# Matmul operands at one address modulo 512 bytes, a second bank for the first gate pair, and transposed factors in the block products of a hybrid encoder layer

## The chip, the cores and the metric

The kernel runs on one core of a Trainium2 chip. The metric is the device time of one execution in microseconds, the median of several runs. A core has TensorE (matrix products, its weight loads shown apart as PEld), VectorE (DVE), ScalarE (ACT), GpSimd (POOL), SyncE (SP, which here issues most transfers), an SBUF of 128 partitions and a PSUM of eight banks of 128x512 f32.

## The reference

One layer over 512 tokens of width 1024, all in float32. Cut to what matters:

```
h = rms_norm(x, attn_norm_g)
(a_q, a_ckv, a_iq, a_ik, a_iw, s5_u, c_qkv, c_z, c_a, c_b, gates) = split(h @ w_in)
y_a = dsa_attention(a_q, a_ckv, a_iq, a_ik, a_iw, ...) @ w_proj_a   # index scores, top-128 keys, softmax
y_b = s5_branch(s5_u, ...) @ w_proj_b             # complex diagonal scan, gelu, GLU with w_glu
y_c = gdn_branch(c_qkv, c_z, c_a, c_b, ...) @ w_proj_c   # chunked delta rule, chunks of 64
g_a, g_b, g_c = split(sigmoid(gates))
x = x + (g_a * y_a + g_b * y_b + g_c * y_c) @ w_out
x = x + (silu(conv(h2 @ w_up)[gate]) * conv(h2 @ w_up)[val]) @ w_down   # h2 = rms_norm(x)
return rms_norm(x, final_norm_g)
```

In the delta rule each chunk solves (m + I) sol = rhs with a strictly lower triangular m of 64x64.

## The kernel before

**Products in float32r.** Every large product is made of three: an operand is split into a rounded part (h) and a remainder (l), and wh·xh, wh·xl and wl·xh are summed in PSUM. A matmul takes a stationary tile of 128x128 and a moving one of 128x512 (`mm`, L248; `tr`, L251, is a transpose). A weight tile of 128x1024 is loaded by `wload` (L273): SyncE's transfer into a staging buffer w (L280), ScalarE's cast to wh (L256), VectorE's subtraction to wl (L257). w has a ring of two buffers and, in the first half, a third buffer in a pool of its own, w3, which `wload` takes for every third load, by the count `self.wi`.

**PSUM.** `acc` (L238) gives a bank from one of four rings: acc has two banks, sm two, pt three, po one.

**Stages.** First the S5 branch's input u is projected from the scaled x (xh, xl), while the norm is made; then the columns of w_in, one tile of 128 after another, from the normalised hh and hl (8 pieces of 128 rows, so 24 matmuls for a tile), in the order of a table PLAN. `ahead` loads tiles two or three in advance. In between run, interleaved, the S5 scan (`s5_half`, L702 to L719 are its complex arithmetic on VectorE), the index scores and top-k of the attention, the DeltaNet (`gdn_main`) and the projections of the finished branches (`merge`, L1328, which reads a branch from f_h and f_l, made by `fetch`, L1306). The output projection (mh, ml), the FFN (f_hh, f_hl and then ah, al) and the last norm follow. A scheduler that orders the instructions of each engine when the program is built decides the places of the interleaved pieces, and the pools decide the addresses: tiles of a pool lie one behind the other in the order in which they are first asked for, and pools on the left side of SBUF behind those opened before.

**Gates.** `gates` (L1313) projects a tile of gate columns, takes the tanh on ScalarE from PSUM (m_th, L1324) and stores it (gd, L1325). The first two tiles of all are made together by `proj_pair` (L350), matmul by matmul, since both wait for hh and hl to arrive piece by piece.

**Block products of the inverse.** `gdn_main` inverts blocks of 32x32 out of 16x16 ones: fifteen steps (L949, L950) give the inverses X of the diagonal blocks; copies arrange them (X1 and X2, L951 to L954); then T1 = ND[:,1]·X1 and X21 = X2·T1 are made as eight pairs of a multiplication of 128x512 (L958) and a sum over its last axis (L959). L958 reads one factor, and of the first product both, with a stride. Xa and Ya gather the blocks and their transposes (L961 to L968) and go through DRAM (g_xd) to give g_X and g_Y (L980), which TensorE multiplies with g_NT.

Of the kernel before, what the change touches and what calls it, by code (L numbers as in the profile page):

```python
# [10 lines left out]
F32 = mybir.dt.float32  # L11
# [160 lines left out]
NBIG = 5  # L172
PLAN = [27, 28, 29, 30, 31, 21, 22, 32, 33, 34, 35, 36, 37, 38, 39, 40, 41, 42, 43, 44, 8, 9, 10, 11, 4, 5, 6, 7, 12, 13, 14, 15,
# [52 lines left out]
class _K:  # L226
# [46 lines left out]
    def wload(self, src, n=1024, hl=None, extra=False):  # L273
        nc = self.nc
        self.wi += 1
        if self.w3 and self.wi % 3 == 0:
            w = self.w3.tile([128, 1024], F32, tag="w3", name="w", bufs=1)
        else:
            w = self.wp.tile([128, 1024], F32, tag="w", name="w", bufs=2)
# [70 lines left out]
    def proj_pair(self, i):  # L350

        self.ahead(2)
        two, pss = [self.fq.pop(0) for _ in range(2)], [self.acc(), self.acc()]
# [266 lines left out]
    def s5_main(self):  # L620
# [4 lines left out]
        for z in range(2):  # L625
# [3 lines left out]
            self.sri.append(x)  # L629
        self.s5q = []  # L630
# [185 lines left out]
    def gdn_main(self):  # L816
# [119 lines left out]
        X, X2, X1, T1, X21 = w3(0, 256, 16), w3(256, 512, 16), w3(512, 640, 8), w3(640, 768, 8), w3(768, 896, 8)  # L936
# [4 lines left out]
        nc.gpsimd.memset(Ya[up, :, h0_], 0.0)  # L941
# [4 lines left out]
        nc.sync.dma_start(ND[up, 1], nv[:, h0_, h1_])  # L946
        for i in range(1, 16):
# [3 lines left out]
        nc.vector.tensor_copy(X1[lo], X[lo, :, 0:8])  # L951
        nc.scalar.copy(X1[up], X[lo, :, 8:16])
# [3 lines left out]
        for dst, a, b in ((T1, ND[:, 1].rearrange("p j i -> p i j"), X1), (X21, X2, T1)):  # L956
            for c in range(0, 16, 4):
                tt(t4, _bc(a[:, c:c + 4], 2, 8), _bc(b.rearrange("p j k -> p k j"), 1, 4), OP.mult)  # L958
                nc.vector.tensor_reduce(dst[:, c:c + 4], t4, AX.X, OP.add)  # L959
        tr_ = lambda x: x.rearrange("p i k -> p k i")  # L960
        nc.scalar.copy(Xa[lo, :, h0_], X[lo])  # L961
        nc.scalar.copy(Xa[up, :, h1_], X[up])
        nc.scalar.copy(Ya[lo, :, h0_], tr_(X[lo]))
# [342 lines left out]
    def fetch(self, d):  # L1306
        h = self.fp_.tile([128, 4, 512], F32R, tag="fh", name="f_h")
        l = self.fp_.tile([128, 4, 512], F32R, tag="fl", name="f_l")
# [48 lines left out]
    def run(self):  # L1357
# [3 lines left out]
        self.sm = ctx.enter_context(self.pool("sm", bufs=2))  # L1361
        self.dp = ctx.enter_context(self.pool("dp", bufs=1, space=DRAM))
# [13 lines left out]
        with ExitStack() as mix:  # L1376
            wst = mix.enter_context(ExitStack())
            self.wp = wst.enter_context(self.pool("wp", bufs=2))
            mpl = mix.enter_context(self.pool("mix", bufs=1))
# [5 lines left out]
            self.ab = mpl.tile([128, 4, 12], F32, tag="ab", name="ab")  # L1385
# [4 lines left out]
            with ExitStack() as s:  # L1390
# [4 lines left out]
                self.s5e = s.enter_context(self.pool("s5e", bufs=1))  # L1395
                hs = ExitStack()
                hp = hs.enter_context(self.pool("hp", bufs=1))
                sync = nc.sync.dma_start
                ag = hp.tile([128, 8], F32, tag="ag", name="ag")
# [298 lines left out]
```

## Time and profile before

| quantity | value |
| --- | --- |
| median of 3 runs | 937.7 us (935.88 to 937.9) |
| profiled execution | 937.33 us, of it span 935.5 us |
| mean granted TensorE clock | 0.992 |
| TensorE busy | 914.2 us, 98% |
| VectorE busy | 646.1 us, 69% |
| ScalarE busy | 414.4 us, 44% |
| GpSimd busy | 62.7 us, 7% |
| moved by DMA | 114.55 MB |

The span is the time from the first to the last instruction of the profiled execution. In the timeline a row is an instruction with its start, its duration, its engine, line and operation, the tile written and the tiles read, and in brackets the idle time of its engine before it and what ended that. Matmuls overlap, so a row of 0.39 us is not a pace: the pace is the distance between two starts. The chain of waits joins instructions that follow each other without a wait into pieces with a count, so duration by count is a pace as well.

### The profile page before, as it was taken

The page shows a single profiled execution, that of the slowest core. Times are in us where ns is not written, and L with a number is a line of the kernel's source. Part 1 is how long each engine was busy: PE and PEld are TensorE (multiplying, and loading weights), DVE is VectorE, ACT ScalarE, POOL GpSimd, SP SyncE. Part 2 cuts the span into 40 slices and gives each one's busy share as a digit, 9 for nine tenths or more (in the row PEclk, how much of TensorE's full clock was granted, in tenths as well). Part 3 has the DMA queues.
Part 4 walks back from the last instruction along what each step waited for, and adds up shares of the span by engine and source line. Part 5 has one row for each costly group of instructions (what it writes and reads, how often), then busy time and mean ns, then how long its engine had stood idle before and what let it go on. Part 6 is the DMA issues. An engine that isn't in the chain of part 4 may idle for free.

```text
span 935.5 us, 12723 instructions
## 1 busy us (share of the span) xinstructions
PE 914.2 (98%) x4804; PEld 744.2 (80%) x4804; DVE 646.1 (69%) x1136; ACT 414.4 (44%) x753; POOL 62.7 (7%) x103
## 2 busy tenths in 40 slices
PE   8989999999999999899999999999999999999996
PEld 6768877788887778788777889888888888888885
DVE  6988498989999779467768545866666666522423
ACT  7467454244575634258733224534443443321212
POOL 3121001021003200400100000000000000000000
PEclk9999999999999999899999999999999999999999
DMA  9585323342335644631147513423223323232312
GB/s 341 179 208 150 105 95 114 119 147 90 101 103 136 166 119 150 191 124 37 45 135 234 205 46 113 136 90 110 94 90 100 103 90 94 87 113 91 103 55 90
DMA packets 48269, 114.55 MB, mean 122 GB/s; under 512 B 13712, under 2 KB 15120, under 8 KB 48080
## 3 DMA queue, kind: packets, MB, share of 16 engines
q1 hardware_dynamic: 40144, 96.76, 32.0%
q0 software_dynamic: 4032, 9.97, 4.4%
q10 hardware_dynamic: 4032, 7.01, 2.1%
q8 instruction: 38, 0.62, 0.3%
q14 instruction: 23, 0.19, 0.1%
HBM read 94.84 MB, written 14.42 MB: 117 GB/s over the span
## 4 chain that ended last, share of the span: by engine, by line
PE 84%; DVE 9%; issue 3%; DMA 2%; ACT 1%; SPq 1%; POOL 0%; POOLq 0%; DVEq 0%; ACTq 0%
PE ps_acc L248 43%; PE ps_sm L248 22%; PE ps_pt L248 13%; PE ps_po L248 4%; DVE wl L257 1%; PE ps_pt L251 1%; DMA sq<-in_x_dram 1%; PE ps_sm L251 1%; DMA w<-in_w_glu_dram 1%; DVE g_xt L958 1%; DVE g_W L959 1%; DVE a_p L1256 0%; DVE s_rd L710 0%; DVE ht L1491 0%; DVE hl L257 0%
## 5 line engine op out<-in xcount | busy, mean ns | idle before, releaser
L257 DVE TENSOR_TENSOR wl<-w,wh 128x1024 fp32r<-128x1024 f32 (+1 forms) x140 | 168.9, 1207 | 137.7 <-ACT wh L256 137.4
L256 ACT CAST wh<-w 128x1024 fp32r<-128x1024 f32 (+1 forms) x140 | 145.5, 1040 | 231.2 <-PE ps_acc L248 126.5
L248 PE MATMUL ps_acc<-hh,wh 128*128 128x512 f32 x376 | 151.2, 402 | 3.4 <-ACT m_th L1324 2.9
L248 PE MATMUL ps_acc<-hh,wl 128*128 128x512 f32 x376 | 150.4, 400 | 0.0
L248 PE MATMUL ps_acc<-hl,wh 128*128 128x512 f32 x376 | 149.2, 399 | 0.0
L248 PEld LDWEIGHTS ps_acc<-hh,wh 128*128 128x128 f32 x376 | 70.9, 188 | 21.4 <-ACT m_th L1324 3.3
L248 PEld LDWEIGHTS ps_acc<-hh,wl 128*128 128x128 f32 x376 | 71.0, 189 | 17.5 <-issue 1.2
L248 PEld LDWEIGHTS ps_acc<-hl,wh 128*128 128x128 f32 x376 | 70.9, 189 | 16.8 <-issue 1.1
L248 PE MATMUL ps_acc<-f_hh,wh 128*128 128x512 f32 x160 | 62.3, 389 | 0.0
L248 PE MATMUL ps_acc<-f_hl,wh 128*128 128x512 f32 x160 | 62.3, 389 | 0.0
L248 PE MATMUL ps_acc<-f_hh,wl 128*128 128x512 f32 x160 | 62.2, 389 | 0.0
L248 PE MATMUL ps_sm<-f_hh,wh 128*128 128x512 f32 x160 | 62.2, 389 | 0.0
L248 PE MATMUL ps_sm<-f_hl,wh 128*128 128x512 f32 x160 | 62.2, 389 | 0.0
L248 PE MATMUL ps_sm<-f_hh,wl 128*128 128x512 f32 x160 | 62.2, 389 | 0.0
L256 ACT CAST ah<-f_th 128x512 fp32r<-128x512 f32 x22 | 13.6, 620 | 57.6 <-DVE f_th L1629 57.6
L248 PEld LDWEIGHTS ps_sm<-f_hh,wh 128*128 128x128 f32 x160 | 30.1, 188 | 6.3
L248 PEld LDWEIGHTS ps_acc<-f_hl,wh 128*128 128x128 f32 x160 | 30.0, 188 | 6.3
L248 PEld LDWEIGHTS ps_sm<-f_hl,wh 128*128 128x128 f32 x160 | 30.0, 188 | 6.2
L248 PEld LDWEIGHTS ps_acc<-f_hh,wl 128*128 128x128 f32 x160 | 30.1, 188 | 6.2
L248 PEld LDWEIGHTS ps_acc<-f_hh,wh 128*128 128x128 f32 x160 | 30.0, 187 | 6.2
L248 PEld LDWEIGHTS ps_sm<-f_hh,wl 128*128 128x128 f32 x160 | 30.0, 187 | 6.2
L1627 ACT ACTIVATE f_th<-f_a 128x512 f32<-128x512 f32 x22 | 13.9, 632 | 45.2 <-DVE f_a L1624 45.2
(553 smaller groups left out, 1941.6 us busy)
## 6 DMA issues: line engine op xcount, KB each, us to landing
w<-in_w_in_dram SPq DMA_DIRECT2D x50, 512.0 KB, 3.5
w<-in_w_up_dram SPq DMA_DIRECT2D x44, 512.0 KB, 3.3
w<-in_w_down_dram SPq DMA_DIRECT2D x22, 512.0 KB, 3.3
gd<-m_th ACTq DMA_DIRECT2D x24, 256.0 KB, 2.1
m_th<-gd SPq DMA_DIRECT2D x24, 256.0 KB, 3.6
w<-in_w_out_dram SPq DMA_DIRECT2D x8, 512.0 KB, 3.9
sq<-in_x_dram SPq DMA_DIRECT2D x4, 512.0 KB, 9.0
w<-in_w_proj_b_dram SPq DMA_DIRECT2D x4, 512.0 KB, 3.8
```

Of the source, the lines that this page charges most:

```text
L248: return self.nc.tensor.matmul(out, lhsT, rhs, start=start, stop=stop)
L251: return self.nc.tensor.transpose(out, in_, self.ident[base:base + n, base:base + n])
L256: self.lasta = nc.scalar.copy(hi, src)
L257: self.lastv = nc.vector.tensor_sub(lo, src, hi.bitcast(F32))
L958: tt(t4, _bc(a[:, c:c + 4], 2, 8), _bc(b.rearrange("p j k -> p k j"), 1, 4), OP.mult)
L959: nc.vector.tensor_reduce(dst[:, c:c + 4], t4, AX.X, OP.add)
L1627: nc.scalar.activation(th, tl[0], AF.Tanh)
```

## The change

- Pads and another order of the pools and tiles (a pad of 112 columns in s5e, a second of 112 in s5, one of 24 on the right side, `ab` in the pool sm, xh and xl first in hp, f_h and f_l allocated once in a pool opened before gs). With them the stationary and the moving operand of nearly all 512-column float32r products begin at the same byte address modulo 512.
- The second tile of the first gate pair takes a bank of the ring pt instead of acc.
- `wload` takes the third staging buffer at another phase of its count.
- In the block products ND[:,1] is first copied in transposed order (NDt, into Ya's place), and X1 and T1 are kept transposed, so that the multiplications read along unit strides. Ya's zeros are written later.

```diff
+S5PAD = 112
@@ wload
-        if self.w3 and self.wi % 3 == 0:
+        if self.w3 and self.wi % 3 == 2:
@@ proj_pair
-        two, pss = [self.fq.pop(0) for _ in range(2)], [self.acc(), self.acc()]
+        two, pss = [self.fq.pop(0) for _ in range(2)], [self.acc(), self.acc("pt")]
@@ s5
+        self.s5.tile([128, 112], F32, tag="pad2", name="s5_pad2", bufs=1)
@@ gdn_main
-        X, X2, X1, T1, X21 = w3(0, 256, 16), w3(256, 512, 16), w3(512, 640, 8), w3(640, 768, 8), w3(768, 896, 8)
+        X, X2, X21 = w3(0, 256, 16), w3(256, 512, 16), w3(768, 896, 8)
+        X1, T1 = w3(512, 640, 16), w3(640, 768, 16)
...
-        nc.gpsimd.memset(Ya[up, :, h0_], 0.0)
...
+        NDt = Ya.rearrange("p (z a) b -> p z (a b)", z=2)[:, 0].rearrange("p (i j) -> p i j", i=16)
+        nc.scalar.copy(NDt, ND[:, 1].rearrange("p j i -> p i j"))
...
-        nc.vector.tensor_copy(X1[lo], X[lo, :, 0:8])
-        nc.scalar.copy(X1[up], X[lo, :, 8:16])
+        tr_ = lambda x: x.rearrange("p i k -> p k i")
+        nc.vector.tensor_copy(X1[lo], tr_(X[lo, :, 0:8]))
+        nc.scalar.copy(X1[up], tr_(X[lo, :, 8:16]))
...
-        for dst, a, b in ((T1, ND[:, 1].rearrange("p j i -> p i j"), X1), (X21, X2, T1)):
+        for dst, a, b in ((tr_(T1), NDt, X1), (X21, X2, T1)):
             for c in range(0, 16, 4):
-                tt(t4, _bc(a[:, c:c + 4], 2, 8), _bc(b.rearrange("p j k -> p k j"), 1, 4), OP.mult)
+                tt(t4, _bc(a[:, c:c + 4], 2, 8), _bc(b, 1, 4), OP.mult)
...
+        nc.gpsimd.memset(Ya[up, :, h0_], 0.0)
@@ fetch
-        h = self.fp_.tile([128, 4, 512], F32R, tag="fh", name="f_h")
-        l = self.fp_.tile([128, 4, 512], F32R, tag="fl", name="f_l")
+        h, l = self.fh
@@ run
+        self.ab = self.sm.tile([128, 4, 12], F32, tag="ab", name="ab", bufs=1)
+        rpad = ctx.enter_context(self.pool("rpad", bufs=1, side="right"))
+        rpad.tile([128, 24], F32, tag="pad", name="rpad")
...
-            mpl = mix.enter_context(self.pool("mix", bufs=1))
...
-            self.ab = mpl.tile([128, 4, 12], F32, tag="ab", name="ab")
...
+                self.s5e.tile([128, S5PAD], F32, tag="pad", name="s5_pad", bufs=1)
...
+                xh = hp.tile([128, 8, 512], F32R, tag="xh", name="xh")
+                xl = hp.tile([128, 8, 512], F32R, tag="xl", name="xl")
...
-                xh = hp.tile([128, 8, 512], F32R, tag="xh", name="xh")
-                xl = hp.tile([128, 8, 512], F32R, tag="xl", name="xl")
...
+                self.fp_ = s.enter_context(self.pool("fob", bufs=1))
+                self.fh = [self.fp_.tile([128, 4, 512], F32R, tag="f" + z, name="f_" + z) for z in "hl"]
                 self.gs = s.enter_context(self.pool("gs", bufs=1))
-                self.fp_ = s.enter_context(self.pool("fob", bufs=1))
```

Where the tiles lie in the two programs, as the pools place them (bytes modulo 512, moving operand less stationary one):

| moving operand | matmuls with 512 columns | before | after |
| --- | --- | --- | --- |
| hh, hl (input projection) | 1,128 | 224 or 416 | 0 |
| mh, ml (output projection) | 192 | 288 | 0 |
| g_oh, g_ol; a_qh, a_ql (with w) | 96; 96 | 320 | 0 |
| xh, xl (u of the S5 branch) | 99 | 192 or 384 | 0 |
| a_ch, a_cl; a_kd, a_kl | 24; 16 | 96 or 192; 416 | 0 |
| f_h, f_l; f_hh, f_hl; ah, al; iq | 96; 960; 528; 8 | 0 | 0 |
| s_glw; g_rows and w_ik | 48; 29 | unequal | unequal |

The equal ones begin at byte 192 of 512 before (iq's at 480), all at 384 after.

The scheduler puts some pieces in other places. On TensorE, at the end of the first gate pair (ps_acc and ps_pt are banks of the two rings, hh and hl the normalised input, wh and wl a weight tile), before:

```order
L248 MATMUL ps_acc<-hh,wh 128x512
L248 MATMUL ps_acc<-hh,wl 128x512
L248 MATMUL ps_acc<-hh,wh 128x512
L248 MATMUL ps_acc<-hh,wl 128x512
L248 MATMUL ps_acc<-hl,wh 128x512 x2
L248 MATMUL ps_acc<-hh,wh 128x512
L248 MATMUL ps_acc<-hl,wh 128x512
```

and now (here ps_pt is the pair's second tile, ps_acc its first or the third tile):

```order
L249 MATMUL ps_pt<-hh,wl 128x512
L249 MATMUL ps_pt<-hl,wh 128x512
L249 MATMUL ps_acc<-hh,wh 128x512
L249 MATMUL ps_acc<-hh,wl 128x512
L249 MATMUL ps_acc<-hl,wh 128x512
L249 MATMUL ps_pt<-hh,wh 128x512
L249 MATMUL ps_pt<-hh,wl 128x512
L249 MATMUL ps_pt<-hl,wh 128x512
L249 MATMUL ps_acc<-hl,wh 128x512
L249 MATMUL ps_acc<-hh,wl 128x512
L249 MATMUL ps_acc<-hh,wh 128x512
```

Before, the last rows of the pair stand ahead of the first row of the third tile; now most matmuls of the third tile stand between those of the pair.

On TensorE, at the first use of g_X, the inverse (a_ch and a_cl are the attention's latent, f_h and f_l the branch that is being merged), before:

```order
L248 MATMUL ps_acc<-wh,a_ch 128x512
L248 MATMUL ps_acc<-wl,a_ch 128x512
L248 MATMUL ps_acc<-wh,a_cl 128x512
L248 MATMUL ps_sm<-g_X,g_NT 128x64 x8
L248 MATMUL ps_acc<-f_h,wh 128x512
L248 MATMUL ps_acc<-f_l,wh 128x512
L248 MATMUL ps_acc<-f_h,wl 128x512
L248 MATMUL ps_acc<-f_h,wh 128x512
```

and now:

```order
L249 MATMUL ps_acc<-f_h,wl 128x512
L249 MATMUL ps_acc<-f_h,wh 128x512
L249 MATMUL ps_acc<-f_l,wh 128x512
L249 MATMUL ps_acc<-f_h,wl 128x512
L249 MATMUL ps_acc<-f_h,wh 128x512
L249 MATMUL ps_acc<-f_l,wh 128x512
L249 MATMUL ps_acc<-f_h,wl 128x512
L249 MATMUL ps_pt<-a_kd,a_qh 128x128
L249 MATMUL ps_sm<-g_X,g_NT 128x64 x8
L249 MATMUL ps_pt<-a_kd,a_ql 128x128
L249 MATMUL ps_pt<-a_kd,a_qh 128x384
```

The eight products of g_X (16 instructions in the trace) stood ahead of the 12 products of the merge's fourth tile (the rows with f_h and f_l into ps_acc); now they stand behind them and behind one product of the attention.

On VectorE, at the end of the block products (m_th of L1344, now L1349, is the merge's multiplication, which reads a bank that TensorE fills), before:

```order
L959 TENSOR_REDUCE g_W<-g_xt 128x32
L809 SCALAR_TENSOR_TENSOR g_k<-g_k,ps_acc 128x512
L257 TENSOR_TENSOR a_wkl<-w,a_wkh 128x512
L965 COPY g_Xa<-g_W 64x16x8
L966 COPY g_Xa<-g_W 64x16x8
L967 COPY g_Ya<-g_W 64x8x16
L968 COPY g_Ya<-g_W 64x8x16
L1344 SCALAR_TENSOR_TENSOR m_th<-m_th,ps_pt 128x512 x2
L257 TENSOR_TENSOR wl<-w,wh 128x512
L1344 SCALAR_TENSOR_TENSOR m_th<-m_th,ps_pt 128x512
```

and now:

```order
L964 TENSOR_TENSOR g_xt<-g_W 128x512
L258 TENSOR_TENSOR a_wkl<-w,a_wkh 128x512
L1349 SCALAR_TENSOR_TENSOR m_th<-m_th,ps_pt 128x512
L965 TENSOR_REDUCE g_W<-g_xt 128x32
L1349 SCALAR_TENSOR_TENSOR m_th<-m_th,ps_pt 128x512
L971 COPY g_Xa<-g_W 64x16x8
L972 COPY g_Xa<-g_W 64x16x8
L973 COPY g_Ya<-g_W 64x8x16
L974 COPY g_Ya<-g_W 64x8x16
L258 TENSOR_TENSOR wl<-w,wh 128x512
L1349 SCALAR_TENSOR_TENSOR m_th<-m_th,ps_pt 128x512
```

Two of the merge's multiplications stood behind the four copies into g_Xa and g_Ya and now stand ahead of them, as does the subtraction a_wkl, which was ahead already.

On SyncE's queue the transfer of the third tile of w_in now stands ahead of all four loads of x (before, behind three of them), and the two transfers of w_glu stand next to each other. The DeltaNet's small preparations (decay, beta and their logarithms and exponentials) now stand near the S5 branch's first steps, ahead of most of the input projection; before, they stood in its middle.

## Rows read from the trace of the kernel before

**Rows 1.** Page: busy time of each engine, share of the span, instructions.

```profile
PE 914.2 (98%) x4804; PEld 744.2 (80%) x4804; DVE 646.1 (69%) x1136; ACT 414.4 (44%) x753; POOL 62.7 (7%) x103
```

**Rows 2.** Chain of waits: start us, duration us, what, xcount.

```profile
28.23 5.05 PE ps_pt L248 x22
...
269.28 5.60 PE ps_acc L248 x24
...
506.53 2.80 PE ps_acc L248 x12
...
595.95 5.44 PE ps_sm L248 x24
```

**Rows 3.** Timeline of TensorE, f_h and f_l, 370 to 375 us.

```profile
370.02 0.39 PE L248 MATMUL ps_pt<-f_h,wl 128*128 128x512 f32 x1
...
374.79 0.40 PE L248 MATMUL ps_pt<-f_l,wh 128*128 128x512 f32 x1
```

**Rows 4.** Timeline of TensorE at the head and the first gate pair.

```profile
21.48 0.50 PE L248 MATMUL ps_pt<-xh,wl 128*128 128x512 f32 x1 [0.58 <-DVE wl L257]
...
53.37 0.50 PE L248 MATMUL ps_acc<-hh,wh 128*128 128x512 f32 x1 [2.85 <-ACT m_th L1324]
...
54.17 0.63 PE L248 MATMUL ps_acc<-hh,wh 128*128 128x512 f32 x1
...
57.58 0.39 PE L248 MATMUL ps_acc<-hh,wl 128*128 128x512 f32 x1
```

**Rows 5.** Timeline of TensorE and ScalarE at the first use of g_X.

```profile
379.10 0.39 PE L248 MATMUL ps_acc<-wh,a_cl 128*128 128x512 f32 x1
...
381.88 3.65 PE L248 MATMUL ps_sm<-g_X,g_NT 128*128 128x64 f32 x16 [2.39 <-DMA g_X<-g_xd]
...
385.28 0.77 PE L248 MATMUL ps_acc<-f_h,wh 128*128 128x512 f32 x1
...
388.77 0.40 PE L248 MATMUL ps_acc<-f_h,wl 128*128 128x512 f32 x1
...
400.25 2.00 PE L248 MATMUL ps_sm<-g_X,g_NT 128*128 128x64 f32 x16
...
402.06 0.31 PE L248 MATMUL ps_pt<-a_kl,a_ql 128*128 128x128 f32 x1
...
379.52 0.59 ACT L1224 COPY a_V<-ps_acc 128x512 f32<-128x512 f32 x1 [0.74 <-PE ps_acc L248]
```

**Rows 6.** Chain of waits at the S5 scan's end and at g_X.

```profile
134.79 0.35 DVE s_rd L705
...
184.53 0.61 DVE s_si L719
...
379.41 2.33 DMA g_X<-g_xd
```

**Rows 7.** Busy us of each engine by stretch, granted clock, DMA share, GB/s.

```profile
50.00:75.00 25.00, 22.15 (x146) 17.63 (x145) 20.80 (x36) 17.19 (x27) 1.52 (x4) 0.93 0.79 201
...
125.00:150.00 25.00, 25.00 (x199) 18.42 (x199) 25.00 (x50) 11.26 (x17) 0.23 (x2) 1.00 0.28 92
...
200.00:225.00 25.00, 25.00 (x110) 20.16 (x109) 25.00 (x54) 10.08 (x18) 3.04 (x6) 1.00 0.28 99
```

**Rows 8.** Line L958: forms, minimum, median and maximum in ns.

```profile
L958 DVE TENSOR_TENSOR g_xt<-g_ND,g_W x4: 1208/1216/1225, 355.4 to 362.3; 128x512 f32<-128x512 f32 x4
...
L958 DVE TENSOR_TENSOR g_xt<-g_W x4: 1160/1178/1205, 364.3 to 371.6; 128x512 f32<-128x512 f32 x4
```

**Rows 9.** Timeline of VectorE, a multiplication with unit strides.

```profile
48.20 0.68 DVE L580 TENSOR_TENSOR s_tb<-s_fh,cst 128x512 f32<-128x512 f32 x1
```

**Rows 10.** Page: cast and subtraction of weight tiles; their loads.

```profile
L257 DVE TENSOR_TENSOR wl<-w,wh 128x1024 fp32r<-128x1024 f32 (+1 forms) x140 | 168.9, 1207 | 137.7 <-ACT wh L256 137.4
...
L256 ACT CAST wh<-w 128x1024 fp32r<-128x1024 f32 (+1 forms) x140 | 145.5, 1040 | 231.2 <-PE ps_acc L248 126.5
...
w<-in_w_in_dram SPq DMA_DIRECT2D x50, 512.0 KB, 3.5
```

More of the change, by code (lines that the diff above doesn't have):

```diff
@@ L955, in gdn_main @@
         t4 = tmp.rearrange("p (i k j) -> p i k j", i=4, k=8)
-        for dst, a, b in ((T1, ND[:, 1].rearrange("p j i -> p i j"), X1), (X21, X2, T1)):
+        for dst, a, b in ((tr_(T1), NDt, X1), (X21, X2, T1)):
             for c in range(0, 16, 4):
-                tt(t4, _bc(a[:, c:c + 4], 2, 8), _bc(b.rearrange("p j k -> p k j"), 1, 4), OP.mult)
+                tt(t4, _bc(a[:, c:c + 4], 2, 8), _bc(b, 1, 4), OP.mult)
                 nc.vector.tensor_reduce(dst[:, c:c + 4], t4, AX.X, OP.add)
-        tr_ = lambda x: x.rearrange("p i k -> p k i")
         nc.scalar.copy(Xa[lo, :, h0_], X[lo])
         nc.scalar.copy(Xa[up, :, h1_], X[up])
+        nc.gpsimd.memset(Ya[up, :, h0_], 0.0)
         nc.scalar.copy(Ya[lo, :, h0_], tr_(X[lo]))
```

## Prediction

> **What bounds the kernel now.** I read the busy times first: TensorE is busy for 914.2 of 935.5 us and VectorE, the next, for 646.1 [rows 1]. So there are two sources of time only: 21 us in which TensorE stands, and the pace at which it goes. For the pace I took runs of equal 128x512 float32r matmuls out of the chain of waits and divided. In the FFN, 24 take 5.44 us, 226.7 ns each; at the input projection 24 take 5.60 us and at the branch projections 12 take 2.80 us, 233.3 ns each [rows 2]. Same shape, same type, same granted clock, and two paces 6.6 ns apart. The stage isn't the reason: in the middle of the busy DeltaNet stage, products that read f_h and f_l start from 370.02 to 374.79 us 21 intervals apart, 227.1 ns each [rows 3].
>
> What parts the two groups is where the pools put the tiles. Of the 3,320 matmuls with 512 float32r columns, those at 226.7 ns have the moving operand and the stationary one at the same byte address modulo 512 (the FFN, f_h/f_l, ah/al); those at 233.3 ns have them 96 to 224 bytes apart, counted the shorter way round. The products of xh and xl stand between, 22 in 5.05 us, 229.5 ns [rows 2]. In the kernel before 1,592 are equal and 1,728 are not. After the change 3,243 are equal; 77 (w_glu's, rsel's, w_ik's) stay as they were.
>
> Then I looked for TensorE's own waits. Two are large and both also cost clock. At the first pair of gate tiles it stands 2.85 us for the tanh of the first tile, and then 8 matmuls from 54.17 to 57.58 us go at 426 ns, which is the 1.2 GHz level [rows 4]. At the first block products of g_X it stands 2.39 us for a load; the 16 small matmuls then take 3.40 us up to the next start against 1.81 us for the same 16 later, and the 8 intervals behind them 3.49 us [rows 5].
>
> **The change, part by part. Addresses.** 1,552 matmuls move from a 233.3 ns placement to an equal one, 99 (xh, xl) from a 229.5 ns one. 1,552 x 6.6 ns = 10.2 us, 99 x 2.8 ns = 0.3 us: 10.5 us if TensorE alone sets the pace. It does not everywhere. Of the 1,552, 1,128 are the input projection (hh, hl), which lies under 300 us. From 135 to 185.1 us the chain runs mainly through VectorE, and its last link there is s_si, for which TensorE waits [rows 6], and in 125 to 150 and 200 to 225 us VectorE is busy 25.00 of 25 us [rows 7] (225 to 275 us reads the same). About 169 unequal matmuls lie in the first of these stretches: what they gain, 1.1 us, is given back in the wait at 185 us. About 306 lie in 200 to 275 us; TensorE has no wait there now, so VectorE is full but not late, and I take back a third of their 2.0 us, 0.7. That leaves 7.4 - 1.8 = 5.6 us. The other 424 (mh/ml of the output projection, g_oh/g_ol, a_qh/a_ql, a few of the attention's) lie from 375 us on, where VectorE has room: 2.8 us, less 0.2 where they stand before a wait. With xh/xl 8.5 us. The ends: 0 if the pace hangs on something else, 10.5 if all is kept.
>
> The row says that equal and unequal addresses differ by 6.6 ns; that it is the address rather than the tile's place in some other sense is my inference from seven pairs of tiles. The Trainium skill speaks against it: SBUF — State Buffer, section "Who interferes with whom", gives TensorE two independent read ports, one for the moving operand and one for the weight load, and says that "PE and ACT never wait on anyone". By that rule the pads would do nothing; that case is the first rival below.
>
> **First gate pair.** The two tiles of the pair were both in the ring of two banks (tag acc), so the third tile's first matmul waited for the tanh of the first to read its bank. With the second tile in the other ring (tag pt) the third takes the free acc bank, and the order shows it between the pair's own matmuls. TensorE is then never without work: 2.85 us of waiting go, and 8 matmuls go at 2.4 GHz, 3.41 - 8 x 0.233 = 1.55 us [rows 4]. Sum 4.4 us. The tanh is late by nothing new; the next user of the acc ring comes a tile, 5.6 us, later. Ends: 2.85, if another short wait keeps the clock down, and 4.4. If VectorE, which carries the chain up to there, delivers the fourth tile's weights late, part returns; that is in the allowance below.
>
> **Block products.** The 8 multiplies take 1.18 to 1.22 us [rows 8] where a multiply of 128x512 with unit strides took 0.68 us [rows 9]. Unit strides save some 8 x 0.5 = 4 us of VectorE; the extra copy NDt is one ScalarE copy of a size that costs well under 1 us, at a time when ScalarE has gaps. None of that is on TensorE's path as such. What moves the time is the order: the 16 matmuls of g_X now stand behind the 12 of the merge's fourth tile. In the trace g_X's data lands at 379.41 + 2.33 = 381.74 us [rows 6]. TensorE is free at 379.10 + 0.23 = 379.33, waits for the bank that a_V's copy leaves at 380.11 [rows 5], some 0.8 us and 0.1 of slow start, and is through the 12 at 380.2 + 12 x 0.227 = 382.9. That is 1.2 us after the data. The faster products would let the data come earlier, but two of the merge's additions now stand before the Xa/Ya copies and wait for TensorE, so I take 381.7 as it is. So 2.39 us of waiting go, 3.40 - 1.81 = 1.59 us of small matmuls at half clock, and 3.49 - 8 x 0.227 = 1.67 us behind them: 5.65, less 0.9, is 4.8 us. Ends: 1.5 (if the data comes 2 us later than before and half of the clock loss stays) and 5.6.
>
> **Head and staging.** The 0.58 us at 21.48 us is a wait for weights whose transfer stood behind a staging buffer [rows 4]; it now takes the third buffer and is issued before the four loads of x. 0.6 us. The rest of the rotation is shifted by a tile. The DeltaNet's small preparations now run some 200 us earlier, in the stretch where VectorE had 20.80 of 25 us [rows 7]; that, three early activation-table loads and all other reordering I can't cost from rows: -2 to +4 us, taken at 1.0 us lost.
>
> **Sum.** 8.5 + 4.4 + 4.8 + 0.6 - 1.0 = 17.3 us. The profiled run took 937.33 us (span 935.5), 0.4 us under the median 937.7: 937.33 - 17.3 = 920.0 us.
>
> **The rivals.**
> First, *the address is not the cause*: the pace of 233 ns belongs to the projections for another reason, or equality at byte 384, where all operands now lie, is not what equality at 192 was. Then 8.5 us fall out, 937.33 - 9.8 + 1.0 = 928.5 us. Against it speak 233.3 ns for several tiles with different distances and 227.1 for f_h in the same stage [rows 2, 3]. 0.05.
>
> Second, *VectorE becomes the bound of the front part*. It is full where TensorE gets faster [rows 7], and carries the chain up to the first gates and to 185 us. Then everything won before 300 us is given back there: what is left is 250 of the hh/hl matmuls behind 295 us (1.65), the 424 (2.6) and g_X (4.8), 9.0 us: 928.3 us. For it: 25.00 of 25 us busy. Against it: TensorE does not wait from 200 to 275 us. 0.16.
>
> Third, *slower: weights starve*. The rotation of staging buffers is shifted, and the two w_glu loads now stand next to each other on SyncE's queue with the input projection's tiles behind them. A tile that is asked for only when TensorE wants it costs its transfer 3.5, cast 1.04 and subtraction 1.21 us [rows 10], 5.75 us, and some 1.6 us at the lower clock: 7.35 us. It decides from 17.3 / 7.35 = 2.4 tiles; three cost 22.05 us, 942.0 us. In the trace no tile starves so: the waits for weights are 0.58 us and below. 0.04.
>
> Fourth, better than forecast: the waits at 185 us and at the end of the attention shrink as well: 914 or less. 0.03.
>
> **How the numbers follow.** The forecast, with the bounds of its terms 914 to 926 us, has 0.72. The first two rivals lie at 928 to 929, so a range from 913 to 930 leaves out the third, part of the fourth and the tails: it should hold 0.85. About 0.2% is what a measurement of this kernel can tell from no change, 1.9 us. Faster by more: forecast, first, second and fourth, 0.96, less 0.03 for a worse mixture of them: 0.93. Same 0.03, slower 0.04.
>
> **What would show it.** Right: x12 and x24 pieces of the chain at 2.72 and 5.45 us in place of 2.80 and 5.60, at the input, branch and output projections alike; no wait for m_th near 50 us and no 426 ns matmuls behind it; no wait for g_X near 380 us, the 16 small ones in about 1.8 us; granted clock near 1.0 in 50 to 75 and 375 to 400 us; the multiplies at about 0.7 us. Wrong: 233 ns anywhere with equal addresses (first rival); TensorE waits for VectorE between 135 and 300 us that sum to over 4 us (second); waits for wl or wh of over 3 us (third).

## The result and the profile after

The changed kernel takes 923.3 us (median of four runs, 921.6 to 927.3) against 937.1 us of the kernel before: a ratio of 0.986, 95% interval 0.9826 to 0.9893. Measured again beside three experiments it took 922.45 us against 937.65 us, 0.984 (0.9824 to 0.9856). The forecast was 920.0 us, between 913 and 930.

The profiled execution after is the slowest of its four: 927.25 us, span 925.5. The second profile of the same program has a span of 919.4 us, 6.1 us less. The two are runs of one program with one order of instructions. Measured from trace to trace (the start of the last FFN product), the first is 10.1 us ahead of the kernel before and the second 16.2; the sum of the prediction was 17.3.

**Pace.** The chain of waits after (start, duration, what, count), at the input projection and at the branch projections:

```profile
252.22 5.47 PE ps_acc L249 x24
...
497.82 2.72 PE ps_acc L249 x12
```

Where 24 matmuls took 5.60 us and 12 took 2.80 [rows 2], they take 5.47 and 2.72: 227.9 and 226.7 ns each. Over all matmuls of hh and hl the mean distance of two starts (those under 245 ns) fell from 233.1 to 227.9 ns, those of mh and ml from 233.1 to 226.9.

**The block products.** TensorE in the timeline after, where before it waited 2.39 us for g_X [rows 5], and the line of the multiplications (minimum, median, maximum in ns):

```profile
373.56 0.39 PE L249 MATMUL ps_acc<-wh,a_cl 128*128 128x512 f32 x1
374.62 0.50 PE L249 MATMUL ps_acc<-f_h,wh 128*128 128x512 f32 x1 [0.68 <-ACT a_V L1230]
...
377.54 1.95 PE L249 MATMUL ps_sm<-g_X,g_NT 128*128 128x64 f32 x16
379.29 0.31 PE L249 MATMUL ps_pt<-a_kd,a_ql 128*128 128x128 f32 x1
```

```profile
L964 DVE TENSOR_TENSOR g_xt<-g_Ya,g_W x4: 684/692/693, 352.2 to 357.5; 128x512 f32<-128x512 f32 x4
L964 DVE TENSOR_TENSOR g_xt<-g_W x4: 684/688/693, 359.0 to 367.1; 128x512 f32<-128x512 f32 x4
```

The wait for g_X is gone, the new one for a_V's bank is 0.68 us (0.8 was expected), the 16 small products take 1.75 us up to the next start where they took 3.40, and nothing goes at half clock behind them. The multiplications take 0.69 us where they took 1.16 to 1.23 [rows 8].

**New waits.** TensorE's waits after (engine, what it waited to write, for whom, us in all, times, longest):

```profile
PE ps_acc L249 <- DVE sp_l L269: 2.2, 1, 2.2
PE ps_acc L249 <- ACT xh L260: 2.1, 1, 2.1
```

The wait for m_th is gone from the list. In its place stand sp_l (the split of the query projection, which frees a bank; 0.55 us before) and xh at the head (1.15 us before). Both cost more than themselves. The head and the query projection in the timeline after:

```profile
10.22 0.50 PE L249 MATMUL ps_acc<-xh,wh 128*128 128x512 f32 x1 [2.09 <-ACT xh L260]
...
11.81 0.62 PE L249 MATMUL ps_acc<-xl,wh 128*128 128x512 f32 x1
...
15.22 0.41 PE L249 MATMUL ps_acc<-xh,wl 128*128 128x512 f32 x1
```

```profile
290.76 0.47 PE L249 MATMUL ps_acc<-hh,wh 128*128 128x512 f32 x1 [2.19 <-DVE sp_l L269]
...
291.80 0.63 PE L249 MATMUL ps_acc<-hl,wh 128*128 128x512 f32 x1
...
295.17 0.39 PE L249 MATMUL ps_acc<-hh,wh 128*128 128x512 f32 x1
```

Behind each, eight matmuls take 3.4 us, 427 ns each, the 1.2 GHz level: 1.6 us more than at 2.4 GHz. The second profile of the same program has the same places with shorter waits, and no such stretch:

```profile
9.62 0.50 PE L249 MATMUL ps_acc<-xh,wh 128*128 128x512 f32 x1 [1.06 <-ACT xh L260]
...
288.05 0.47 PE L249 MATMUL ps_acc<-hh,wh 128*128 128x512 f32 x1 [1.34 <-DVE sp_l L269]
```

The windows tell the same, first the first profile, then the second (busy us and instructions of PE, PEld, DVE, ACT, POOL; granted clock, DMA share, GB/s):

```profile
0.00:25.00 25.00, 20.81 (x86) 16.96 (x87) 15.49 (x54) 16.76 (x26) 9.19 (x15) 0.93 0.90 338
275.00:300.00 25.00, 22.81 (x104) 18.33 (x103) 21.14 (x51) 12.53 (x26) 7.63 (x14) 0.93 0.53 129
400.00:425.00 25.00, 25.00 (x209) 20.56 (x209) 14.55 (x43) 17.40 (x43) 0.00 (x0) 0.93 0.23 72
```

```profile
0.00:25.00 25.00, 21.41 (x94) 17.05 (x95) 16.08 (x59) 16.98 (x27) 9.22 (x15) 1.00 0.90 337
275.00:300.00 25.00, 23.66 (x115) 19.20 (x114) 23.25 (x52) 13.55 (x25) 10.35 (x18) 1.00 0.64 164
400.00:425.00 25.00, 25.00 (x223) 21.36 (x222) 16.63 (x49) 21.00 (x55) 0.00 (x0) 1.00 0.13 44
```

In the first profile three windows have a clock of 0.93, in the second none. The 6.1 us between them are these: 1.9 at the head (wait and clock together), 2.4 at the query projection, 1.5 around 401 us, where TensorE had no wait but ran small products of 64 and 32 columns, and 0.3 in smaller places.

### The profile page after: what moved, and what is told of

Its sections match the earlier page's. It is cut to its first block, busy times and chain, and to the rows that moved or that the text cites. A ratio compares the mean times of both kernels' runs of the same rounds, so it can differ in the third digit from the quotient of the medians.

```text
span 925.5 us, 12717 instructions
## 1 busy us (share of the span) xinstructions
PE 905.5 (98%) x4804; PEld 744.5 (80%) x4804; DVE 640.5 (69%) x1136; ACT 413.2 (45%) x752; POOL 65.0 (7%) x103
## 4 chain that ended last, share of the span: by engine, by line
PE 86%; DVE 8%; issue 2%; DMA 2%; ACT 1%; POOL 1%; SPq 0%; POOLq 0%; DVEq 0%; ACTq 0%
PE ps_acc L249 44%; PE ps_sm L249 22%; PE ps_pt L249 14%; PE ps_po L249 4%; PE ps_pt L252 1%; DVE wl L258 1%; PE ps_sm L252 1%; DMA w<-in_w_glu_dram 1%; DMA xt<-in_xt_dram 1%; DMA a_ql<-sp_h 1%; DVE a_wk L1141 1%; DVE g_v L798 0%; DVE a_m L1140 0%; DVE s_rb L711 0%; POOL g_orr L371 0%
## 5 line engine op out<-in xcount | busy, mean ns | idle before, releaser
L249 PE MATMUL ps_acc<-hh,wh 128*128 128x512 f32 x368 | 146.0, 397 | 2.2 <-DVE sp_l L269 2.2
L249 PE MATMUL ps_acc<-hl,wh 128*128 128x512 f32 x368 | 145.6, 396 | 0.0
L249 PE MATMUL ps_acc<-hh,wl 128*128 128x512 f32 x368 | 145.4, 395 | 0.0
L1636 ACT ACTIVATE f_th<-f_a 128x512 f32<-128x512 f32 x22 | 13.9, 632 | 45.2 <-DVE f_a L1633 45.2
```

The source lines that it names most:

```text
L249: return self.nc.tensor.matmul(out, lhsT, rhs, start=start, stop=stop)
L1636: nc.scalar.activation(th, tl[0], AF.Tanh)
```

## The experiments

Twelve kernels ran, four at a time on one chip; each ratio is against runs of the kernel before on that chip. The one with matmuls alone ran once and has no ratio. A difference between two kernels of under 2 us lies within the spread of their runs.

### The changed kernel again

> The changed kernel once more, as the yardstick on the chip of the three runs beside it. Expected: 921 to 925 us. Theory A (the profiled run of 927 us was slow because TensorE fell to 1.2 GHz in three stretches, of which only those behind a wait belong to the kernel): the profile shows the waits for xh near 8 to 10 us and for sp_l near 288 us again, with 8 matmuls at 427 ns behind each, but not necessarily the stretch near 401 us, behind which no wait lies. Theory B (all three belong to the program): all three stretches at the same places.

Measured 922.45 us (0.984). The rows are above. Theory A holds, and goes further than it said: the stretches at 1.2 GHz behind the two waits do not belong to the program either. The same program waited 2.19 or 1.34 us for sp_l, 2.09 or 1.06 us for xh, and only the longer ones were followed by half clock.

### hh and hl moved by 128 bytes

```diff
-        rpad.tile([128, 24], F32, tag="pad", name="rpad")
+        rpad.tile([128, 56], F32, tag="pad", name="rpad")
```

> The changed kernel with the right-hand pad 128 bytes wider. The order of the instructions on every engine is the same; only hh, hl and the two tiles beside them move by 128 bytes, so the 1,128 matmuls of hh and hl have their operands 128 bytes apart again. Theory (address decides the pace): those go from about 227.5 to 233 ns, 1,128 x 5.5 to 6.6 ns = 6 to 7.4 us of TensorE, less up to 1.8 us that VectorE hides: 4.5 to 7 us slower than the changed kernel beside it, pieces of 24 in the chain at 5.60 us where they are 5.45. Rival (the pace belongs to the projections' order or stage): the same time as the changed kernel and 227 ns.

Measured 928.82 us (0.9904, 0.9889 to 0.9919), 6.4 us slower than the changed kernel beside it (give or take 2). The order on all five engines is unchanged, so the addresses alone did it. The chain, first of this kernel, then of the changed one at the same tile:

```profile
254.61 5.58 PE ps_acc L249 x24
```

```profile
250.36 5.47 PE ps_acc L249 x24
```

5.58 us is 232.5 ns, 5.47 is 227.9. Over all matmuls of hh and hl the mean rose from 227.9 to 232.6 ns; those of f_h and f_l, which did not move, had 228.3 and now 229.0. The rival of the wrong cause falls. One thing in the expectation is not so: more moved than hh, hl and two tiles. In the changed kernel this pad stays to the end, and mh and ml, which later take the same side of SBUF, lie 128 bytes off as well: their mean rose from 226.8 to 232.7 ns. 1,128 x 4.7 = 5.3 us and 192 x 5.9 = 1.1 us make the 6.4, so no part hidden by VectorE is seen here.

### hh and hl brought to the weights' address in the kernel before

```diff
             right = ExitStack()
+            right.enter_context(self.pool("rpad", bufs=1, side="right")).tile([128, 72], F32, tag="pad", name="rpad")
```

> The kernel before with one pad of 72 columns on the right-hand side and nothing else: the order on all engines is that of before, but for 960 of the 1,128 matmuls of hh and hl both operands now begin at byte 192 of 512; the other 168 stay 192 bytes apart. Theory (address): 960 matmuls at 227 ns, 6.3 us less of TensorE; about 1.5 us of that hidden by VectorE before 300 us; 4.5 to 6.3 us faster than before, near 931 to 932.5 us; the waits for m_th and g_X of before stay. Rival (address does nothing, the gain of the changed kernel is all from its waits): 937 us.

Measured 934.35 us against 937.65 (0.996, 0.9944 to 0.9975): 3.3 us faster with nothing but a pad, and below the 4.5 us expected; the order is again unchanged. The mean of hh and hl fell from 233.1 to 228.3 ns, 1,128 x 4.8 = 5.4 us of TensorE (this pad is gone before mh and ml come, and they stay at 233.1). So 2.1 us of these, two fifths, did not arrive; by the interval it is between 0.2 and 3.1 us.

The trace does not put this down to VectorE alone. The lead is 1.3 us at 161 us. From 164.2 to 167.4 us the matmuls then go at 1.2 GHz, which they do not in the trace of before, and TensorE is 0.8 us behind. At the S5 scan's last products (186 us) it is 0.6 us ahead again, since the wait of 0.92 us for s_sr at 184.6 us is gone. The lead is 1.7 us before the wait for sp_l (293 us) and 1.4 behind it: here VectorE takes its share, as the second rival says. What it would have taken at 185 us without the lower clock, this trace does not tell.

### Matmuls alone, by distance

> Only matmuls of 128x128 by 128x512 in float32r, back to back, in groups of 32 with no other work: the tile's name tells how many bytes the moving operand lies behind the stationary one modulo 512 (d000 to d480 in steps of 32, d004, d016), then groups with both at one address with another base (b064 to b448), and 224 and 0 once more. All of the layer's computation is left out. Theory (the distance modulo 512 decides): 0 and all bases at 226.7 to 227 ns, 7.26 us for 32; all other distances at 233 ns or between, 7.46 us. Rival 1 (the base decides, or the pair of tiles): groups b differ among themselves. Rival 2 (it needs other engines that use the memory at the same time): all groups at one pace, 227 ns.

The chain, one piece for each group of 32 (start, duration, name, count; the name's number is the distance in bytes, b and e as above):

```profile
19.60 7.25 PE d000x L38 x32
26.85 7.47 PE d032x L38 x32
34.32 7.33 PE d064x L38 x32
...
49.13 7.47 PE d128x L38 x32
...
71.56 7.46 PE d224x L38 x32
79.02 7.28 PE d256x L38 x32
...
93.77 7.33 PE d320x L38 x32
...
138.47 7.58 PE d004x L38 x32
146.05 7.42 PE d016x L38 x32
...
189.92 7.29 PE b384x L38 x32
...
204.51 7.46 PE e224x L38 x32
211.97 7.27 PE e000x L38 x32
```

At distance 0 a matmul takes 226.6 ns and at 224 bytes 233.1, with no other engine at work and back again at the end: rival 2 falls. All seven other bases took 7.27 to 7.29 us: rival 1 falls too, and base 384 is as good as 192. But two points of the theory were wrong. 256 bytes is as good as 0 (227.5 ns), 64 and 320 are equal to each other and lie between (229.1 ns), and all other multiples of 32 take 7.46 to 7.49 us: what counts is the distance modulo 256, not 512. And 4 bytes is worst of all, 236.9 ns. The unequal distances were tried at one base only.

By this the table under "The change" cannot be right as it is headed: g_oh stands there at 320, which is 229.1 ns here, and has 233.2 ns in the trace of before; xh stands at 192 or 384, which are both 233.4, and has 229.5 in rows 2. The table counts the other way round, stationary less moving, and mh, which it lists as moving, is the stationary operand of its products (`mm3`), with w moving. The pads say the same: the 24 columns on the right side are 96 bytes and bring hh to byte 384, so it lay at 480, where iq lies, and 480 less the weights' 192 is 288, not 224. The single steps from start to start show it too, since each distance has a pattern of its own:

| matmuls alone: distance, steps in ns | kernel before: operands, distance turned round, steps in ns |
| --- | --- |
| 288: 231, 235, 233, 234 | hh, hl: 288; 231, 235, 233, 234 (from 270 us) |
| 224: 232, 235, 232, 235 | mh, ml: 224; 232, 235, 232, 235 (from 530 us) |
| 192: 231, 236, 231, 236 | g_oh, g_ol: 192; 231, 236, 231, 236 (from 486 us) |
| 320: 229, 232, 226 | xh, xl, most tiles: 320; 229, 232, 226 (from 14 us) |
| 128: 238, 229, 238, 229 | xh, xl, one tile: 128; 238, 229, 238, 229 (from 22 us) |

So the rule found with matmuls alone holds in the kernel, distance by distance, and the 229.5 ns of xh and xl, which the prediction took from rows 2 without a reason, belong to a tile at 320.

### The third tile of w_in later

```diff
-XO = 'w0,t0,w0,t1,w1,t2,t3,w2,x0,x1,x2,x3'
+XO = 'w0,t0,w0,t1,w1,t2,t3,x0,x1,x2,w2,x3'
```

> The changed kernel with the third tile of w_in asked for behind the third load of x, as in the kernel before (in the changed one it is ahead of all four). Theory (that transfer delays the second pair of xt, so that TensorE waits 2.1 us for xh near 8 us where it waited 1.15 before, and falls to 1.2 GHz for 8 matmuls): the wait falls to about 1.2 us, the first matmuls stay at full clock, 1 to 2.7 us less up to the end of the first projection, and near 920 to 922 us in all. Rival (the order of the queue doesn't matter; the transfers share the same 16 engines anyway): the wait stays over 2 us, and the time is that of the changed kernel. The scheduler moves other pieces too, so the whole time may differ by 1 to 2 us for other reasons; the start up to 40 us is what decides.

Measured 922.28 us, the changed kernel's time. The waits for xh, from the timeline of this kernel:

```profile
8.17 0.50 PE L249 MATMUL ps_acc<-xh,wh 128*128 128x512 f32 x1 [0.33 <-ACT xh L260]
...
10.21 0.49 PE L249 MATMUL ps_acc<-xh,wh 128*128 128x512 f32 x1 [0.52 <-ACT xh L260]
```

The wait went from one of 1.1 to 2.1 us into pieces of 0.5 and less, and the clock stays up there; but the products of the third tile then stand late again at 21 us, and the first product of hh starts at 39.0 us, between the changed kernel's 39.3 and 37.5 of its two profiles. The transfer's place moves the wait; the whole gains nothing. The rival's result came, by the theory's mechanism. This trace has matmuls at 1.2 GHz elsewhere, from 149 to 152 us, behind waits of 0.57 and 0.96 us with small products between them; what they cost in all is not separated.

### The gate pair in one ring again

```diff
-        ... [self.acc(), self.acc("pt")]
+        ... [self.acc(), self.acc()]
```

> The changed kernel with both tiles of the first gate pair in the ring of two banks again. Theory: TensorE waits for the tanh near 50 us again (2 to 3 us) with 8 matmuls at 427 ns behind it: 3 to 4.5 us slower than the changed kernel, 926 to 928 us. Rival (VectorE carries the chain there, so the gain was given back at once): less than 1 us slower. The scheduler moves about a fifth of the rows by a place or more, so the stretch from 38 to 70 us decides, not the total alone.

Measured 918.59 us (0.981, 0.9791 to 0.9829): not slower at all, rather faster than the changed kernel's 0.984. The theory falls. TensorE's wait in this kernel:

```profile
52.66 0.50 PE L249 MATMUL ps_acc<-hh,wh 128*128 128x512 f32 x1 [1.41 <-ACT m_th L1329]
```

It waits 1.41 us, not 2.85, and no matmul behind it goes at half clock. ScalarE shows why. First the kernel before, then the changed one (second profile), which has g_bet ahead of the cast too:

```profile
51.42 1.28 ACT L1324 ACT_TABLE_LOAD   x1
52.72 0.60 ACT L1324 ACTIVATE m_th<-ps_acc 128x512 f32<-128x512 f32 x1
```

```profile
50.06 1.28 ACT L843 ACT_TABLE_LOAD   x1
51.35 0.21 ACT L843 ACTIVATE g_bet<-ab 128x16 f32<-128x16 f32 x1
51.48 1.04 ACT L257 CAST wh<-w 128x1024 fp32r<-128x1024 f32 x1
52.42 0.58 ACT L1329 ACTIVATE m_th<-ps_acc 128x512 f32<-128x512 f32 x1
```

Before, the table of the tanh was loaded between the last cast and the first tanh, on the path. In the changed kernel a small activation of the DeltaNet (g_bet), moved here by the scheduler, has loaded it ahead of the cast. So with the activation moved, 1.44 us of the wait and the 1.55 us of half clock are gone already, and the other ring has 1.4 us left to win at its place. In "The other ring in the kernel before" it is the other way round: the activation has not moved, and the ring alone takes the whole wait. At the end nothing of that is to be seen: undoing it moved other pieces too, and the wait for sp_l does not appear in this kernel.

### The block products as before

```diff
-        X1, T1 = w3(512, 640, 16), w3(640, 768, 16)
-        nc.scalar.copy(NDt, ND[:, 1].rearrange("p j i -> p i j"))
-        for dst, a, b in ((tr_(T1), NDt, X1), (X21, X2, T1)):
+        X1, T1 = w3(512, 640, 8), w3(640, 768, 8)
+        for dst, a, b in ((T1, ND[:, 1].rearrange("p j i -> p i j"), X1), (X21, X2, T1)):
...
```

> The changed kernel with the block products as before (strided factors, Xa and Ya as before); addresses, gate pair and staging as changed. Theory (the gain at g_X comes from the order, 16 small matmuls behind the 12 of the merge, and not from the faster multiplications): if the order on TensorE stays as in the changed kernel, the wait for g_X stays away or below 1 us, and the time is within 1.5 us of the changed kernel. Rival (the faster multiplications bring the data in time): TensorE waits 2 to 4 us for g_X near 375 us, with half clock behind it, 3.5 to 5 us slower.

Measured 927.63 us (0.9897), 4 to 5 us slower than the changed kernel. The scheduler put g_X back ahead of the merge's tile, and the wait is back:

```profile
377.38 3.58 PE L249 MATMUL ps_sm<-g_X,g_NT 128*128 128x64 f32 x16 [2.50 <-DMA g_X<-g_xd]
```

The wait and the time are the rival's, but the faster products and the order went together. What the slower multiplications cost the data can be read: VectorE's copies into g_Xa start at 371.11 us, in the changed kernel's first profile at 370.62. Half a microsecond does not make a wait of 2.50 us; that the order makes it, the next kernel shows.

### The new block products in the kernel before

The diff above the other way round, in the kernel before.

> The kernel before with the new block products alone (transposed factors, the extra copy, the later zeros); addresses, gate pair and staging as before. The scheduler then sets the 16 small matmuls of g_X behind the 12 of the merge's fourth tile, as in the changed kernel. Theory: the wait of 2.4 us for g_X goes, with the half clock behind it, against a wait of some 0.8 us for a bank: 3.5 to 4.8 us faster than before, 932.5 to 933.8 us; the waits for m_th at the first gate pair and the pace of 233 ns stay. Rival (the data of g_X comes later by as much, or the DeltaNet's chain behind it sets the pace): within 1.5 us of before.

Measured 932.93 us against 936.86 (0.9957, 0.9942 to 0.9972): 3.9 us faster. The timeline:

```profile
380.09 0.50 PE L248 MATMUL ps_acc<-f_h,wh 128*128 128x512 f32 x1 [0.68 <-ACT a_V L1228]
...
383.01 1.95 PE L248 MATMUL ps_sm<-g_X,g_NT 128*128 128x64 f32 x16
```

No wait for g_X, 0.68 us for the bank, full clock: the theory, with its size. And the data came no earlier, though the multiplications take 0.69 us here. VectorE's copy into g_Xa, first in the kernel before, then in this one:

```profile
375.73 0.22 DVE L965 COPY g_Xa<-g_W 64x128 f32<-64x128 f32 x1
```

```profile
376.04 0.22 DVE L969 COPY g_Xa<-g_W 64x128 f32<-64x128 f32 x1
```

The four loads of g_X land from 380.94 to 383.02 us, in the kernel before from 380.51 to 382.75. So it is the order, the 12 products of the merge ahead of the 16 of g_X, that removes the wait, and not the faster multiplications; they matter by what the scheduler makes of them.

### The other ring in the kernel before

```diff
-        ... [self.acc(), self.acc()]
+        ... [self.acc(), self.acc("pt")]
```

> The kernel before with the second tile of the first gate pair in the ring pt and nothing else by hand; the scheduler then also moves the first small matmuls of g_X behind part of the merge. Theory (the sum's step for the pair): the wait of 2.85 us for m_th and the eight matmuls at 427 ns go, 4.4 us less at 87 us of the trace; with VectorE's chain up to 185 us at most half is given back. In all 933 us, or 929 us if the wait for g_X goes too. Rival (VectorE carries the chain from 38 to 185 us, and takes it back): less than 1 us is left at 186 us.

Measured 927.16 us against 936.86 (0.9899): 9.7 us, more than the 933 or 929 us expected. In its trace TensorE has no wait near 50 us and no matmul at half clock behind it, although the table of the tanh is loaded as late as before:

```profile
53.56 1.28 ACT L1324 ACT_TABLE_LOAD   x1
54.86 0.60 ACT L1324 ACTIVATE m_th<-ps_acc 128x512 f32<-128x512 f32 x1
```

Counted by matmuls of hh and hl, it leads by 4.1 us where the kernel before stands at 83 us: the 4.4 us of the sum, by the ring alone. New is a wait of 1.41 us for the index queries at 94.8 us. At the last product of hh (368.4 us before) it leads by 5.1 us, and behind the DeltaNet (456 us) by 10.7: 5.6 us come from g_X, whose small products now stand in pieces behind the merge. The line edited stands at 50 us; more than half of what it brought came from the scheduler 320 us later.

### Only addresses and pool order

```diff
-        if self.w3 and self.wi % 3 == 2:
+        if self.w3 and self.wi % 3 == 0:
-        ... [self.acc(), self.acc("pt")]
+        ... [self.acc(), self.acc()]
```

and the block products as before, all in the changed kernel.

> The changed kernel with gate pair, staging and block products all as before: what is left is the pads, the order of the pools and what the scheduler makes of them. Theory A (the parts add up): faster than before by the addresses alone, 8.5 us, 929 us, since the waits at the gate pair and at g_X come back. Theory B (the places that the scheduler gives to the pieces decide the waits, and these have already moved here: g_X stands behind part of the merge, the activation tables are loaded earlier): no wait over 2 us at the gate pair or at g_X, and near 920 to 923 us, though no line was written for it.

Measured 920.93 us (0.984, 0.9818 to 0.9862): the time of the whole change, with gate pair, staging and block products all as before. Theory B holds: without a line written for them, both waits are small or gone. TensorE and VectorE in its timeline:

```profile
52.10 0.50 PE L249 MATMUL ps_acc<-hh,wh 128*128 128x512 f32 x1 [1.41 <-ACT m_th L1325]
```

```profile
368.26 0.78 PE L249 MATMUL ps_sm<-g_X,g_NT 128*128 128x64 f32 x6
...
369.83 0.39 PE L249 MATMUL ps_acc<-wh,a_cl 128*128 128x512 f32 x1
```

```profile
358.99 0.22 DVE L967 COPY g_Xa<-g_W 64x128 f32<-64x128 f32 x1
```

The wait at the gate pair is the short one, and g_X is multiplied without a wait, although the multiplications are strided as before (1.14 to 1.18 us each): they are done by 359 us, 11 us ahead of the last product of a_cl, where the kernel before copies Xa only at 375.7 us, 3.4 us ahead of it.

### The query projection in two rings

```diff
-            ps = self.proj(W_Q + n)
+            ps = self.proj(W_Q + n, "pt" if n % 2 else "acc")
```

> The changed kernel with the second and fourth tile of the query projection in the PSUM ring pt instead of acc. In the changed kernel TensorE waits 2.2 us near 288 us for sp_l, which frees a bank of the ring acc, and then goes 8 matmuls at 427 ns: 3.7 us together, against 0.55 us before. Theory (the bank is what it waits for): wait and half clock go, 2.5 to 3.7 us faster than the changed kernel, near 919.5 to 921 us. Rival (VectorE and ScalarE are late there altogether, ScalarE behind a transfer from GpSimd's queue): the wait moves to the next weights or to the next user of a bank, and the time stays within 1 us.

Measured 928.95 us (0.9915), 6 us slower than the changed kernel. The wait for sp_l is gone, and this is what came instead:

```profile
321.05 1.16 PE L249 MATMUL ps_pt<-g_k 128*128 128x128 f32 x8 [1.85 <-DVE g_v L930]
```

Behind it eight matmuls go at half clock, and between 286 and 297 us it waits three times for weights, up to 0.91 us. VectorE is late there altogether, as the rival says, though neither had the time right: 919.5 to 921 us by the theory, within 1 us of the changed kernel by the rival. The order at the block products changed as well; its share isn't separated.

### The fastest with the later tile

The gate pair in one ring and the third tile later, both diffs above in the changed kernel.

> The kernel that was fastest so far (the changed one with both tiles of the gate pair in the ring of two, 918.6 us) with the third tile of w_in asked for behind the third load of x. Theory (the wait for xh near 8 us, 2.3 us there, costs 8 matmuls at 427 ns besides itself): with the wait in pieces below 1 us TensorE stays at full clock, 1 to 2 us less, 916.5 to 917.5 us. Rival (the wait for the weights of the third tile near 20.5 us and other places by the scheduler take it back): 918.5 us or more.

Measured 918.91 us (0.9813, 0.9796 to 0.983): no gain over 918.59. The wait for xh is 1.02 us and no matmul goes at half clock at the head; the trace has a span of 916.9 us, but the median says the rival: 918.5 us or more.

## Why the prediction was right, point by point

**Addresses: right in mechanism, near in size; the period is 256 bytes.** The pace of hh and hl fell by 5.2 ns in place of 6.6. In the second profile after, the first nine steps behind an interruption are 228 to 233 ns on the mean, and from the tenth on they are 226.5 to 227.3; why they start slower is not shown. Moving hh and hl off, with mh and ml, cost 6.4 us in the changed kernel, of which 5.3 are hh and hl by their pace; bringing 960 of them on gave 3.3 in the one before; the term for hh and hl was 5.6. For the output projection and the query products beside it the two traces give 1.9 and 2.0 us between 496 and 565 us for 288 matmuls, 6.5 to 7.0 ns each. What VectorE takes back was set at a quarter. In the kernel before two fifths did not arrive, part of it by a lower clock at 164 us; in the changed kernel no missing part is seen. What in the chip makes the distance matter, no run shows.

**g_X: right.** 4.8 us were set, 3.9 measured alone; the new wait was 0.68 us where 0.8 was written. The step on which it rests, that the data comes when it came before and only the order changes, is borne out by the copies at 376.04 and 375.73 us.

**Gate pair: right, with a second cause not seen.** The wait and the half clock are gone, and the ring alone takes them away in the kernel before: 4.1 us in its trace where 4.4 was set. But the step "both were in the ring of two banks, so the third tile waited" missed that ScalarE's own delay made up half of this wait. The row for it, the load of the tanh's table, stands 1.3 us ahead of the tanh in the trace of before and was not read; the early table loads were in the text only as a risk. In the changed kernel that load has moved, and without the ring it takes 3.0 of the 4.4 us, as the kernel with the pair in one ring shows. The two are different ways to the same wait and must not be added.

**Head: wrong.** 0.6 us was booked as a gain, because the transfer of the third tile goes ahead. That wait did go, but the same transfer stands ahead of the loads of x, and the wait for xh near 10 us was 1.06, 1.37, 1.71, 1.93, 2.09 and 2.31 us in six profiles with that order, against 1.14, 1.15, 1.18, 1.67 and 1.72 us in five with the old one. Four of the six were followed by half clock, none of the five. That the transfer is the cause is likely from the run with the later tile, where it came in pieces of 0.5 us, but the spread within each group is nearly as large as the difference.

**New waits: right place, too small.** 1.0 us was allowed. The wait for sp_l alone is 1.3 or 2.2 us against 0.55, and costs another 1.6 when the clock falls. What makes sp_l late was not separated. The medians lie 2.5 and 3.3 us above the forecast, and these waits and the head are the terms that came out worse than set.

**The sum held because its total was read from the built order, not because the parts add.** The parts alone gave 3.3 (hh and hl), 3.9 (block products) and 9.7 us (ring): 16.9 us; the pads and pools alone gave 15.9, and everything together 13.9 and 15.2, the same within the intervals. They are different ways to the same few waits. Only the pads that left the order as it was, 3.3 and 6.4 us, show a gain that stands by itself.

**The rivals.** Weights did not starve: no wait for wl or wh is among the longer ones after. TensorE lost part of the front's gain where it waits for VectorE, at 185 us and at the query projection: 4.5 us in the first profile, 1.6 of them by the lower clock, and 2.3 in the second; not all of it. The first rival, that the address is not the cause, fell with the two pads that left the order as it was.

## What to carry to other kernels

Where two runs of the same matmul differ in pace by a few ns, compare the addresses of the moving and the stationary operand: a pad costs a few hundred bytes of a partition. The two pads on the right side changed no instruction's place; the pads and the new order of the pools together changed many, so compare the built order each time. Where a scheduler sets the order, an edit's gain is not at the edited line; read the waits of the whole built program, and undo single edits before crediting them. A wait of TensorE is to be priced with the clock that may fall behind it, and a wait of about 2 us that varies from run to run spreads the times by the same stretch.

## What the runs showed of the hardware

- The distance of two starts of a 128x512 float32r matmul depends on the distance of its two operands modulo 256 bytes: 226.6 ns at 0, 227.5 at 256, 229.1 at 64 and 320, 233.1 to 234.1 at the other multiples of 32 up to 480, 231.9 at 16, 236.9 at 4. No other engine is needed for it, and the kernel's own steps have the same patterns. The unequal distances were measured with the stationary operand at one base. The Trainium skill, as quoted in the prediction (SBUF — State Buffer, "Who interferes with whom"), calls the two reads independent. The pace here is not independent of the two addresses; whether it is the reads that meet is not shown.
- Behind waits of TensorE of 1.71, 1.83, 1.85, 1.93, 2.01, 2.09, 2.19, 2.31, 2.39, 2.45, 2.50 and 2.85 us the clock fell to 1.2 GHz for seven or more matmuls; behind waits of 1.02, 1.06, 1.34, 1.37, 1.41, 1.67 and 1.72 us it stayed at 2.4 GHz.
- The clock also fell without a wait of that length: around 401 us of the first profile after, behind products with 64 and 32 columns, and not in the second profile of the same program; at 164 us of the kernel before with the pad of 72 columns, behind waits of 0.49 and 0.65 us with small products between them, and not at the same place of the kernel before.
- A load of a ScalarE table took 1.28 us, and the activation behind it started 1.30 us after the load's start.
- A VectorE multiplication of 128x512 f32 with one or two strided inputs took 1.14 to 1.23 us, with unit strides (and one broadcast dimension) 0.69.
